# A decoder layer on one core: inputs laid depth-first, the norm applied to the products, and the large projections by Strassen's seven products

## The chip, the cores and the metric

The kernel runs on one core of a Trainium2 chip. The metric is the device time of one execution in microseconds (us), lower is better. The core has five engines that work side by side and wait for each other by semaphores: PE multiplies matrices and writes to PSUM banks of 128 x 512 fp32, DVE and ACT are the vector and the scalar engine, POOL is GpSimd, and SP here does nothing but issue DMAs. Each engine works off its own list of instructions in order.

## The reference

One layer of a decoder, in fp32, with 1024 rows of x and a width of 2048:

```python
h = rmsnorm(x, norm_mix)
(sb_q, sb_k, sb_v, sb_g, gla_q, gla_k, gla_v, gla_r, gla_g, sgu_u, sgu_v, sgu_g) = split(h @ w_in)
o_sb  = stick_breaking_attention(sb_q, sb_k, sb_v)          # 8 heads of 128, strictly causal
o_gla = gla_chunked(gla_q, gla_k, gla_v, log_alpha(gla_r))  # 4 heads
o_sgu = chunked_sgu(gelu(sgu_u), gelu(sgu_v))               # 4 groups of 128
mix = rmsnorm per head of concat(o_sb, o_gla, o_sgu)
x = x + (mix * silu(concat(sb_g, gla_g, sgu_g))) @ w_out
x = x + memory_cross_attention(rmsnorm(x, norm_xattn), rmsnorm(mem, norm_mem))
return rmsnorm(x, final_norm)
```

`w_in` is 2048 x 7184 and `w_out` 2048 x 2048; the memory has 256 rows. In the attention each score row becomes log-probabilities through a running sum from the right end (`suffix`), which is masked so that a row sees only earlier columns.

## The kernel before, in words

**Two parts for each operand.** Every large fp32 operand is split into a float32r tile and the remainder (`split_to`, L142: an ACT cast, L143, then a DVE subtraction, L144). A product of two such pairs is three matmuls (`mm3`, L184). Weights come in pieces of 128 x 512 (256 KB) through `raw_weights` L150 (3 buffers `wraw`) and `weights` L159 (3 buffers `whl` for the two parts). The order of PE's list is written by hand: `weave` (L224) lays the groups of a projection (one weight piece, and the matmuls that use it) in a row and puts each small task before the step that its due time names.

**Stages.** (1) Rows of x arrive, are normed on DVE (L348), and are turned by PE (`flip`, L179) into `hT`, 16 slices of 128 along the depth by two halves of 512 rows, as two parts; meanwhile the first columns of v are computed. (2) `natural` / `row_block` (L269, L242) compute the rest of v, the GLA values and gate and the three SGU inputs, with one k-slice of a 512-column weight at a time into 8 banks; results go to DRAM scratch. (3) Keys and values of the memory. (4) `column_block` (L195) computes transposed products for 128 columns: four groups, each of one weight piece and 24 matmuls. Through it run the gates, GLA's q and k (beside them the SGU tasks, then the GLA tasks from L576 on, whose seven levels per pair of heads are DVE work in `gla_decay`, `gla_factors`, `gla_level`), then q and k of each attention head, always one head ahead of the tasks of `attend` (L831). (5) The output projection goes in four chunks of 512 columns (`mixed` L956 makes the operand from the heads' results and gates, `evac_chunk` L973 adds x). (6) The second norm, the cross-attention and the last norm.

**The attention tasks.** `scores` (L847): three matmuls for a tile of z, then ACT abs, exp and ln (L858 to L860), DVE (L861), for the tile on the diagonal a DVE multiplication by a triangle of ones (L863), the running sum on DVE (L865), a copy of its end on POOL (L869), a DVE subtraction (L871), ACT exp (L872), and a POOL `affine_select` on the diagonal tile (L844). `turn` (L877) transposes the probabilities, `values` (L891) multiplies by v, which POOL's own DMA queue brings (L838), `square` and `close` (L899, L909) norm the head.

**POOL** has little in its list besides: one product of gate and mixer in SGU (L543), GLA (L749) and `mixed` (L970).

```python
def zero_later(dsl):
    pool.affine_select(out=dsl, in_=dsl, pattern=[[-1, P]], compare_op=ALU.is_gt, fill=0.0,
                       base=0, channel_multiplier=1)
...
act.activation(tw, tw, AF.Ln, bias=1.0)
dve.scalar_tensor_tensor(out=tw, in0=z, scalar=0.0, in1=tw, op0=ALU.max, op1=ALU.add)
if diag:
    dve.tensor_tensor(out=t[:, width - P:width], in0=t[:, width - P:width], in1=consts["before"], op=ALU.mult)
```

Of the kernel before, what the change touches and what calls it, by code (L numbers as in the profile page):

```python
# [34 lines left out]
def spread(ap, n):  # L35
    """[p, a] -> [p, a, n], each value n times."""
    p, a = ap.shape
    return ap.unsqueeze(2).to_broadcast([p, a, n])
# [3 lines left out]
def trunk(ctx, tc, x, mem, norm_mix, w_in, w_gla_gate_up, b_gla_gate, sgu_norm, w_sgu, b_sgu,  # L42
          out_norm, w_out, norm_xattn, norm_mem, w_xq, w_xkv, w_xo, final_norm, out, dbg=None):
# [3 lines left out]
    x2d, mem2d, out2d = x[0], mem[0], out[0]  # L47
    w_in3 = w_in[0].rearrange("(k p) n -> p k n", p=P)
# [6 lines left out]
    actp = ctx.enter_context(tc.tile_pool(name="actp", bufs=16))  # L55
    wraw = ctx.enter_context(tc.tile_pool(name="wraw", bufs=3))
# [11 lines left out]
    def slot(dt=F32R, name="slot"):  # L68
        return actp.tile([P, 4, 512], dt, tag="act", name=name)

    class Operand:
        """[2048, 1024] with its first axis on partitions, as two tiles that add up to it, by four k and half."""
# [4 lines left out]
        def fill(self, half):  # L77
            for kg in range(4):
                self.t[kg, half] = (slot(), slot())
# [4 lines left out]
        def group(self, kg, s):  # L84
            c = (s % 4) * P
            return tuple(t[:, :, c:c + P] for t in self.t[kg, s // 4])

    def scratch(name, shape):
# [4 lines left out]
    ident = const.tile([P, P], F32, name="ident")  # L93
    make_identity(nc, ident)
    ones_f = const.tile([P, P], F32, name="ones_f")
    dve.memset(ones_f, 1.0)
    ones_r = const.tile([P, P], F32R, name="ones_r")
    dve.tensor_copy(ones_r, ones_f)
    eps_t = const.tile([P, 1], F32, name="eps_t")
    dve.memset(eps_t, EPS)  # L100

    layout = (("out", out_norm[0], 16), ("xat", norm_xattn[0], 16), ("mem", norm_mem[0], 16), ("bg", b_gla_gate[0], 2),
              ("bs", b_sgu[0], 4))
    cols_at, n_cols = {}, 0
    for nm, _, n in layout:
        cols_at[nm] = n_cols
        n_cols += n
    cols = const.tile([P, n_cols], F32, name="cols")

    def load_cols():  # L110
        """Vectors that act per partition, one column for each 128 values."""
        rows = wraw.tile([P, 512], F32, tag="wr", name="rows")
        for nm, src, n in layout:
            c = cols_at[nm]
# [80 lines left out]
    def column_block(acts, w3, c0, evac, halves=(0, 1)):  # L195
# [6 lines left out]
        def step(kg, kk):  # L202
# [10 lines left out]
            if k == KT - 1:  # L213
                for h in halves:
                    evac(h, banks[h])
# [1003 lines left out]
```

## Time and profile before

| what | value |
|---|---|
| three runs | 2186.28, 2185.3, 2181.64 us; median 2185.3 us |
| profiled execution | span 2184.6 us from the first to the last instruction |
| busy share of the span | PE 97%, DVE 47%, ACT 39%, POOL 7% |
| moved by DMA | 231.18 MB, 106 GB/s over the span |

The profile's span is the nearest figure to a run's time; it lies 0.7 us below the median. "Busy" counts an instruction from its start to its end, and matmuls overlap in PE's pipeline, so a busy PE is not always a PE at full pace. A row of groups names line, engine, operation, output and input, shapes and count, then the busy time in us and the mean of one in ns, then idle time ahead of them and what ended it.

### The profile page before, as it was taken

Reading aid. Unit: us, or ns where it says so; the run is one execution under the profiler, and the core shown is the slowest. Engines: PE = TensorE matmul, PEld = TensorE weight load, DVE = VectorE, ACT = ScalarE, POOL = GpSimd, SP = SyncE. Lnnn points to the kernel's source line nnn. Section 1 sums busy time; section 2 is a strip of 40 time slices with the busy share of each in tenths; the row PEclk is TensorE's granted clock in tenths of the full one; section 3 lists DMA queues with packets and bytes.
Section 4 is the critical chain, followed back from the end, with each engine's and each line's share of the span. In section 5 each row is a group of like instructions: output and inputs, shape, how many; then the busy total and the mean of one; then the engine's idle time right before and its main releaser. Section 6 shows DMA issues by size and latency. Waiting matters only on the chain.

```text
span 2184.6 us, 28465 instructions
## 1 busy us (share of the span) xinstructions
PE 2125.8 (97%) x10525; PEld 1767.4 (81%) x10525; DVE 1020.7 (47%) x1984; ACT 860.9 (39%) x1987; POOL 163.5 (7%) x273
## 2 busy tenths in 40 slices
PE   6999999999999999999999999999989999999997
PEld 6998888888887767878888888888877878888885
DVE  6621211111115627375377677776753121377674
ACT  6421111221215424242356565666654121356552
POOL 2110000000000110101111111111012000000001
PEclk9999999999999999999999999999999999999999
DMA  7541321331317621313222222222267231655632
GB/s 215 151 146 49 126 87 49 97 97 49 98 55 219 184 61 44 107 34 92 78 57 55 56 63 56 61 54 56 83 192 231 69 124 49 207 201 154 216 121 92
DMA packets 181847, 231.18 MB, mean 106 GB/s; under 512 B 17270, under 2 KB 106956, under 8 KB 179532
## 3 DMA queue, kind: packets, MB, share of 16 engines
q1 hardware_dynamic: 170572, 214.68, 32.1%
q0 software_dynamic: 11136, 14.69, 2.6%
q8 instruction: 83, 1.36, 0.3%
q14 instruction: 56, 0.46, 0.1%
HBM read 177.93 MB, written 51.38 MB: 105 GB/s over the span
## 4 chain that ended last, share of the span: by engine, by line
PE 44%; DVE 8%; ACT 5%; issue 4%; DMA 2%; POOL 1%; DVEq 0%; SPq 0%; POOLq 0%; ACTq 0%
PE pj L175 31%; PE z L175 6%; PE av L175 4%; PE tr L180 1%; DVE a L865 1%; DVE a L871 1%; PE tr L175 1%; ACT a L872 1%; DMA mraw<-mix 1%; ACT t L859 1%; ACT t L860 1%; DVE t L861 1%; DVE ql L663 1%; ACT t L858 1%; DVE wl L144 1%
## 5 line engine op out<-in xcount | busy, mean ns | idle before, releaser
L144 DVE TENSOR_TENSOR wl<-wr,wh 128x512 fp32r<-128x512 f32 (+1 forms) x392 | 267.6, 683 | 773.8 <-ACT wh L143 767.6
L175 PE MATMUL pj<-slot,wh 128*128 128x512 f32 x2048 | 576.9, 398 | 1.6 <-DVE qT L144 1.6
L143 ACT CAST wh<-wr 128x512 fp32r<-128x512 f32 (+1 forms) x395 | 237.6, 602 | 798.4 <-PE av L175 548.6
L175 PE MATMUL pj<-wh,slot 128*128 128x512 f32 (+1 forms) x1760 | 500.7, 370 | 0.0
L175 PEld LDWEIGHTS pj<-slot,wh 128*128 128x128 f32 x2048 | 369.7, 188 | 72.4 <-issue 2.3
L175 PEld LDWEIGHTS pj<-wh,slot 128*128 128x128 f32 x1760 | 321.5, 190 | 54.8
L175 PE MATMUL pj<-wl,slot 128*128 128x512 f32 (+1 forms) x880 | 328.9, 374 | 1.7 <-DVE wl L144 1.5
L175 PE MATMUL pj<-slot,wl 128*128 128x512 f32 x1024 | 327.9, 391 | 0.0
L175 PEld LDWEIGHTS pj<-slot,wl 128*128 128x128 f32 x1024 | 192.2, 188 | 42.7
L175 PEld LDWEIGHTS pj<-wl,slot 128*128 128x128 f32 x880 | 167.1, 190 | 30.3 <-DVE wl L144 2.3
L175 PE MATMUL z<-wh,slot 128*128 128x512 f32 x576 | 178.6, 390 | 0.7 <-DVE slot L144 0.7
L175 PEld LDWEIGHTS z<-wh,slot 128*128 128x128 f32 x576 | 108.2, 188 | 24.1 <-DVE slot L144 1.9
L175 PE MATMUL z<-wl,slot 128*128 128x512 f32 x288 | 112.5, 391 | 4.4 <-DVE xo L982 2.7
L861 DVE SCALAR_TENSOR_TENSOR t<-z,t 128x384 f32<-128x384 f32 (+2 forms) x96 | 53.4, 556 | 94.3 <-ACT t L860 94.2
L872 ACT ACTIVATE a<-a 128x384 f32<-128x384 f32 (+2 forms) x96 | 50.4, 525 | 114.5 <-DVE a L871 114.4
L175 PE MATMUL pj<-slot,oT 128*128 128x512 f32 x384 | 92.7, 396 | 0.0
L175 PE MATMUL tr<-wh,slot 128*128 128x512 f32 x288 | 88.7, 389 | 0.0
L175 PE MATMUL av<-wh,slot 128*128 128x512 f32 x288 | 88.7, 389 | 0.0
L175 PEld LDWEIGHTS pj<-slot,oT 128*128 128x128 f32 x384 | 71.0, 188 | 15.7
L175 PE MATMUL z<-kT,qT 128*128 128x512 f32 (+3 forms) x288 | 71.1, 355 | 0.0
L175 PEld LDWEIGHTS z<-wl,slot 128*128 128x128 f32 x288 | 54.0, 188 | 17.2 <-DVE xo L982 3.6
L144 DVE TENSOR_TENSOR aTl<-tr,aTh 128x512 fp32r<-128x512 f32 (+2 forms) x112 | 55.2, 493 | 19.3 <-ACT aTh L143 18.2
(252 smaller groups left out, 2684.2 us busy)
## 6 DMA issues: line engine op xcount, KB each, us to landing
wr<-in_w_in_dram SPq DMA_DIRECT2D x216, 256.0 KB, 2.8
wr<-in_w_out_dram SPq DMA_DIRECT2D x88, 256.0 KB, 2.8
xt<-in_x_dram SPq DMA_DIRECT2D x32, 256.0 KB, 4.8
wr<-in_w_xkv_dram SPq DMA_DIRECT2D x32, 256.0 KB, 3.2
v<-v_scr POOLq DMA_DIRECT2D x64, 128.0 KB, 2.8
xr<-in_x_dram SPq DMA_DIRECT2D x32, 256.0 KB, 5.1
x<-xo SPq DMA_DIRECT2D x32, 256.0 KB, 4.4
x2t<-x SPq DMA_DIRECT2D x8, 1024.0 KB, 7.2
```

The costliest lines, as they stand in the source:

```text
L143: act.copy(hi, src)
L144: eng.tensor_tensor(out=lo, in0=src, in1=f32(hi), op=ALU.subtract)
L175: i = pe.matmul(o, l, r, start=start, stop=stop)
L180: i = pe.transpose(o, i_, ident)
L663: dve.tensor_tensor(out=gl["ql"][r_, :, hh, :].rearrange("p c (b i) -> p c b i", i=h), in0=gl["q"][r_, :].rearrange("p (c b i) -> p c b i" ...
L858: act.activation(tw, z, AF.Abs)
L859: act.activation(tw, tw, AF.Exp, scale=-1.0)
L860: act.activation(tw, tw, AF.Ln, bias=1.0)
L861: dve.scalar_tensor_tensor(out=tw, in0=z, scalar=0.0, in1=tw, op0=ALU.max, op1=ALU.add)
L865: dve.tensor_tensor_scan(out=aw[:, ::-1], data0=tw[:, ::-1], data1=tw[:, ::-1], initial=init, op0=ALU.add, op1=ALU.max)
L871: dve.tensor_tensor(out=aw, in0=z, in1=aw, op=ALU.subtract)
L872: act.activation(aw, aw, AF.Exp)
```

## The change

**Layout.** Three inputs are handed over in another layout: x and memory also with the depth first (`xT`, `memT`), and the short vectors as columns. PE no longer turns x, memory or the vectors. The rms factors are computed beside the first products and applied to the results (`r_all` along the columns, `r_row` and `r_mem` per row). Only the gains are applied to x when a slice is loaded.

**Seven products.** Both operands of a projection are cut into quarters: rows of x in two halves, depth in two halves, columns of the weight in two halves. Strassen's scheme computes seven products of sums of quarters instead of eight products of quarters. `products` (new L290) runs one product over 8 k-slices for two blocks of columns. For each k-slice it loads one or two 128 x 512 weight quarters, adds or subtracts them on POOL (L308), splits the sum (L153 ACT, L154 DVE) and multiplies. `x_load` and `x_sum` (L377, L384) make the operand of the other side, one per round. `Block.evac` adds the products to accumulators in SBUF. v, SGU u and v, GLA v and GLA q, k go this way in seven rounds (products 5, 1, 7, 6, 3, 2, 4).

**Pairs.** The q and k of each of the eight heads, and the 16 gates as eight pairs of 128 columns, go through `pair_steps` (L611) in three sweeps over all 16 pairs: products 2 and 4 (kind 24), 3 and 5 (kind 35), 1, 7 and 6 (kind 176). Sums of weights are on POOL: 128 x 256 (L636) in the first two sweeps, 128 x 384 (L640) in the third. Half-done results wait in DRAM (`part_scr`). `finish` (L558) multiplies by the rms factor on POOL (L559), and for gates forms the silu by three ACT passes and a second POOL product (L565). SGU and GLA tasks run beside the first two sweeps, the attention beside the third, the memory projection and the first rounds of the output projection, which has seven rounds of two blocks of columns (products 7, 4, 2, 3, 5, 1, 6) with accumulators that start as x.

**Smaller edits.** The mask of the scores goes from a DVE product to a second `affine_select` on POOL (L1055). `close` multiplies by ones in plain fp32 instead of two float32r parts, and multiplies by the gate on POOL (L1125). The raw weight buffers go from 3 to 8, the big operand slots from 16 to 8.

```diff
-    wraw = ctx.enter_context(tc.tile_pool(name="wraw", bufs=3))
+    wraw = ctx.enter_context(tc.tile_pool(name="wraw", bufs=8))
...
+    def products(units, sums, spread_out):
...
+        def load(j):
+            for i in range(0 if not j else j + 1, min(j + 2, len(units))):
+                fetch(i)
+            bl, i, k = units[j]
+            r, n = raw.pop(j), bl.width
+            if len(r) == 2:
+                pool.tensor_tensor(out=r[0][:, :n], in0=r[0][:, :n], in1=r[1][:, :n], op=plus_minus(OF_W[i][1][2]))
+            tw[j] = tuple(whl.tile([P, 512], F32R, tag=f"w{x_}", name=f"w{x_}") for x_ in "hl")
+            split_to(tw[j][0][:, :n], tw[j][1][:, :n], r[0][:, :n])
...
+    def x_sum(i, r, pool_, first=False):
...
+            if first and (i, sh, kh) in SQUARED:
+                sq = ev1.tile([P, 512], F32, tag="sq", name="sq")
+                act.activation(sq, t, AF.Square)
+                pool.tensor_tensor(out=squares[:, sh], in0=squares[:, sh], in1=sq, op=ALU.add)
+        if i in (6, 7):
+            pool.tensor_tensor(out=ps[0], in0=ps[0], in1=ps[1], op=ALU.subtract)
+        if i in (1, 2, 5):
+            act.activation(ps[0], ps[0], AF.Copy, scale=g[0])
+            dve.scalar_tensor_tensor(out=ps[1], in0=ps[1], scalar=g[1], in1=ps[0], op0=ALU.mult, op1=ALU.add)
+            split_to(hi, lo, ps[1])
+        else:
+            split_gain(hi, lo, ps[0], g[0])
...
+    PHASES = (5, 1, 7, 6, 3, 2, 4)
...
+    def finish(t, dst, half, silu):
+        pool.tensor_tensor(out=t, in0=t, in1=r_all[:, half * 512:half * 512 + 512], op=ALU.mult)
+        if silu:
+            e = ev_tile()
+            act.activation(e, t, AF.Exp, scale=-1.0)
+            act.activation(e, e, AF.Ln, bias=1.0)
+            act.activation(e, e, AF.Exp, scale=-1.0)
+            pool.tensor_tensor(out=t, in0=t, in1=e, op=ALU.mult)
+        sp.dma_start(dst[:, half * 512:half * 512 + 512], t)
...
+    def evac_176(n, b, st):
+        _, to, silu = PAIRS[n]
+        m1 = ev_tile()
+        act.copy(m1, b[1])
+        for q, i in enumerate((7, 6)):
+            dve.tensor_tensor(out=st[q], in0=b[i], in1=st[q], op=ALU.add)
+        for q in range(2):
+            pool.tensor_tensor(out=st[q], in0=st[q], in1=m1, op=ALU.add)
+            finish(st[q], to[q], q, silu)
...
+            if nk == 2:
+                pool.tensor_tensor(out=t[:, :256], in0=t[:, :256], in1=t[:, 256:], op=ALU.subtract)
+            else:
+                r = t
+                t = ev.tile([P, 3 * P], F32, tag="ts", name="ts", bufs=2)
+                pool.tensor_tensor(out=t, in0=r[:, :3 * P], in1=r[:, P:], op=ALU.add)
+            tw[j] = tuple(whl.tile([P, 512], F32R, tag=f"w{x_}", name=f"w{x_}") for x_ in "hl")
+            split_to(tw[j][0][:, :width], tw[j][1][:, :width], t[:, :width])
...
             if diag:
-                dve.tensor_tensor(out=t[:, width - P:width], in0=t[:, width - P:width], in1=consts["before"], op=ALU.mult)
+                zero_later(t[:, width - P:width])
...
-            for i in range(2):
-                mm(st, ones_r, t[:, i, :], i == 0, i == 1)
+            mm(st, ones_f, sq, True, True)
...
+            pool.tensor_tensor(out=sq, in0=sq, in1=gt, op=ALU.mult)
...
-        natural(mT, w_out3, n * 512, 512, evac_chunk(n), order=order)
+    PHASES_O = (7, 4, 2, 3, 5, 1, 6)
```

POOL's list before, in the attention stage: loads of v (L838), the select on the probabilities (L844) and the copy of a running sum's end (L869) are all there is.

```order
L838 DMA v<-v_scr_92 128x256
L844 AFFINE_SELECT a<-a 128x128 x4
L869 COPY carry<-a 128x1
L838 DMA v<-v_scr_93 128x256
L838 DMA v<-v_scr_94 128x256
```

POOL's list now, in the attention stage, at the end of a pair of gates (`ts` is a sum of weights on its way to PE, `ev` results on their way to DRAM, `sq` a head's normed output, `gt` its gate, `t` and `a` the scores' tiles):

```order
L640 TENSOR_TENSOR ts<-wr 128x384
L604 TENSOR_TENSOR ev<-ev 128x512
L559 TENSOR_TENSOR ev<-ev,r_all 128x512
L604 TENSOR_TENSOR ev<-ev 128x512
L559 TENSOR_TENSOR ev<-ev,r_all 128x512
L640 TENSOR_TENSOR ts<-wr 128x384
L565 TENSOR_TENSOR ev<-ev 128x512 x2
L1047 DMA v<-v_scr_90 128x256
L1055 AFFINE_SELECT t<-t 128x128
L640 TENSOR_TENSOR ts<-wr 128x384
```

The weight sums now stand in one list with the results' products, with two selects for each diagonal tile instead of one, and with the loads of v; the sum for the next weight piece stands behind whatever is ahead of it there.

PE's list before, beside an attention head's values (`pj<-slot` are the projection's matmuls, `av` the values', `tr` the transposes of the probabilities, `z` the scores):

```order
L175 MATMUL pj<-slot,wl 128x512 x2
L175 MATMUL av<-aTl,v 128x256
L175 MATMUL av<-aTh,v 128x256 x2
L175 MATMUL av<-aTl,v 128x128
L175 MATMUL av<-aTh,v 128x128 x2
L175 MATMUL pj<-slot,wh 128x512 x4
```

PE's list now, at such a place:

```order
L185 MATMUL pj<-wh,slot 128x512 x2
L185 MATMUL av<-aTl,v 128x256
L185 MATMUL av<-aTh,v 128x256 x2
L185 MATMUL av<-aTl,v 128x128
L185 MATMUL av<-aTh,v 128x128 x2
L185 MATMUL z<-kT,qT 128x512 x3
L185 MATMUL pj<-wl,slot 128x512
```

The attention's own matmuls are the same; a weight piece now feeds 9 matmuls (three products of one k-slice) where it fed 24.

982 lines of the change are left out of this document (566 added, 416 removed).

## The prediction

> **What bounds the kernel now.** I read the page first, then the clock, then the busy time by stage, then the chain of waits in a stage that looks full, then single stretches of DVE and POOL. The page:
>
> ```profile
> span 2184.6 us, 28465 instructions
> PE 2125.8 (97%) x10525; PEld 1767.4 (81%) x10525; DVE 1020.7 (47%) x1984; ACT 860.9 (39%) x1987; POOL 163.5 (7%) x273
> GB/s 215 151 146 49 126 87 49 97 97 49 98 55 219 184 61 44 107 34 92 78 57 55 56 63 56 61 54 56 83 192 231 69 124 49 207 201 154 216 121 92
> core 0: 2184.6 us, clock 0.996
> ```
>
> The busy time by stage (after the engines: granted clock, DMA share, GB/s):
>
> ```profile
> core 0: us, PE busy (x) PEld busy (x) DVE busy (x) ACT busy (x) POOL busy (x), PEclk, DMA share, GB/s
> 0.00:50.00 50.00, 33.69 (x238) 31.73 (x239) 31.65 (x68) 32.30 (x88) 13.17 (x17) 0.97 0.72 218
> 50.00:100.00 50.00, 48.86 (x408) 47.72 (x409) 34.14 (x83) 25.30 (x74) 6.51 (x10) 1.00 0.54 160
> 100.00:700.00 600.00, 598.71 (x2758) 496.57 (x2757) 111.14 (x185) 127.42 (x226) 7.23 (x12) 1.00 0.32 96
> 775.00:1045.00 270.00, 262.12 (x1314) 210.73 (x1313) 149.29 (x237) 87.75 (x177) 28.91 (x41) 1.00 0.23 66
> 1045.00:1550.00 505.00, 501.67 (x2584) 419.63 (x2583) 340.42 (x653) 296.49 (x660) 61.12 (x155) 1.00 0.23 60
> 1550.00:1665.00 115.00, 107.15 (x492) 86.13 (x491) 63.84 (x106) 62.18 (x121) 22.38 (x21) 0.99 0.56 178
> 2170.00:2185.00 15.00, 0.57 (x3) 0.13 (x1) 4.56 (x9) 1.85 (x5) 1.69 (x1) 0.66 0.18 70
> ...
> 105.00:125.00 20.00, 20.00 (x169) 19.94 (x168) 8.30 (x20) 6.61 (x18) 3.67 (x6) 1.00 0.57 167
> ```
>
> PE is the bound in every stage; DVE reaches two thirds only in the first 100 us and in the attention (340 of 505), and POOL does nothing worth naming: 61 of 505 us there. The kernel has no waits left that could pay for a rewrite; a gain can only come from fewer matmuls. What one costs is seen where PE's chain is unbroken:
>
> ```profile
> 1859.09 54.40 PE pj L175 x240
> ```
>
> That is 54.40 / 240 = 0.227 us for 512 columns; the stretch from 105 us, all of 256 columns, gives 20 / 169 = 0.118, say 0.12.
>
> **What PE loses.** Counted in the two orders, 512-column float32r matmuls fall from 7696 to 6880, 256-column ones from 1456 to 1296, transposes from 732 to 572; 32 256-column matmuls in plain fp32 come on top (the heads' norms). Per transpose and per fp32 matmul:
>
> ```profile
> L180 PE MATMUL tr<-ident,a 128*128 128x128 f32 x288 | 44.5, 273 | 0.0
> L175 PE MATMUL z<-v,kdn 128*128 128x256 f32 x28 | 8.4, 380 | 0.0
> ```
>
> The transposes' busy share is 44.5 / 288 = 0.155 us each, an upper bound since their ends overlap; 128 columns at the pace of 0.227 for 512 would be 0.057, a lower one, and I take 0.1. So: 816 x 0.227 = 185, 160 x 0.12 = 19, 160 x 0.1 = 16, less 32 x 0.38 = 12 and about 3 of small ones: **-205 us**. Strassen saves an eighth of the large projections; that is all of it.
>
> Waits of replaced stages go too. In the first 100 us PE handles 646 matmuls, mostly of 256 columns, where the full rate of 169 in 20 us would need 76; after about 10 us of start it had 90, so 14 were lost. GLA's stretch leaves 270 - 262 = 8, the start of the output projection 115 - 107 = 8. Together **-30**, and 2184.6 - 205 - 30 = 1950 would be the span if every new instruction hid.
>
> **What the others gain.** POOL goes from some 150 us of work to some 950, SP from 865 DMAs to 2315, moved bytes by two. POOL's part matters because it does not run beside DVE freely. DVE and POOL around 720 us, then around 1641 us:
>
> ```profile
> 719.84 0.74 DVE L524 SCALAR_TENSOR_TENSOR sv<-sv,rs_r,gn 128x512 f32<-128x512 f32 x1
> 720.50 1.77 DVE L144 TENSOR_TENSOR wl<-wr,wh 128x512 fp32r<-128x512 f32 x1
> ...
> 720.06 1.66 POOL L543 TENSOR_TENSOR y<-y,sg 128x512 f32<-128x512 f32 x1 [570.56 <-ACT wh L143]
> ```
>
> ```profile
> 1640.57 0.69 DVE L144 TENSOR_TENSOR slot<-mraw,slot 128x512 fp32r<-128x512 f32 x1 [2.83 <-ACT slot L143]
> 1641.62 1.38 DVE L144 TENSOR_TENSOR wl<-wr,wh 128x512 fp32r<-128x512 f32 x1 [0.35 <-ACT wh L143]
> ...
> 1641.15 1.29 POOL L970 TENSOR_TENSOR mraw<-mraw,graw 128x512 f32<-128x512 f32 x1 [1.26 <-ACT graw L969]
> ```
>
> The split that takes 0.69 alone takes 1.77 beside a POOL product, and ends 0.55 after it: the two exclude each other, they do not slow each other. Likewise the POOL product that meets a DVE instruction takes 1.66, not 1.29. So in each stage POOL's tensor instructions and DVE's with two inputs in SBUF form one queue, and where that queue is longer than PE's work, it is the bound. Its prices:
>
> ```profile
> L749 POOL TENSOR_TENSOR og<-og,gg 128x256 f32<-128x256 f32 x16 | 13.4, 841 | 102.8 <-ACT v L748 102.8
> L844 POOL TENSOR_SCALAR_AFFINE_SELECT a<-a 128x128 f32<-128x128 f32 x64 | 19.3, 301 | 193.2 <-ACT a L872 184.1 <-PE pj L175 9.0
> L869 POOL COPY carry<-a 128x1 f32<-128x1 f32 x32 | 9.6, 301 | 139.4 <-DVE a L865 139.4
> L144 DVE TENSOR_TENSOR wl<-wr,wh 128x512 fp32r<-128x512 f32 x360 | 254.1, 706 | 746.4 <-ACT wh L143 740.2 <-DMA xr<-in_x_dram 4.8 <-PE tr L180 0.6
> L144 DVE TENSOR_TENSOR wl<-wr,wh 128x256 fp32r<-128x256 f32 x32 | 13.6, 424 | 27.4 <-ACT wh L143 27.4
> L871 DVE TENSOR_TENSOR a<-z,a 128x384 f32<-128x384 f32 x16 | 8.8, 552 | 2.3 <-POOL carry L869 2.3
> L865 DVE TENSOR_TENSOR_SCAN a<-t,carry 128x512 f32<-128x512 f32 x32 | 41.0, 1281 | 0.6
> L865 DVE TENSOR_TENSOR_SCAN a<-t 128x384 f32<-128x384 f32 x16 | 15.3, 957 | 1.0
> ```
>
> *Seven rounds of w_in.* A round is 240 x 0.227 + 96 x 0.12 = 66 us of PE. The third has 16 weight sums of 512 (1.29) and 16 of 256 (0.84), 8 differences of x and 8 sums of squares on POOL, 55 in all, and 32 splits and 8 of x on DVE, 24: 79, or 12 too long. The first, with 24 sums of squares, is 72. The others lie under 66. **+18** (0 to 40).
>
> *Pairs 24 and 35, with SGU and GLA.* A level of GLA takes PE 1.5 units of 12 matmuls, 18 x 0.227 = 4.1, and 16 small ones of its own, 846.68 - 844.90 = 1.8 by the first two rows here. DVE needs the others:
>
> ```profile
> 844.90 2.02 PE L175 MATMUL z<-ql,d 128*128 128x128 f32 x16
> 846.68 1.18 PE L175 MATMUL pj<-slot,wh 128*128 128x512 f32 x4
> ...
> L653 DVE TENSOR_TENSOR d<-bc 128x1024 f32<-128x1024 f32 x14 | 16.8, 1220 | 0.2
> L663 DVE TENSOR_TENSOR ql<-q,d 64x512 f32<-64x512 f32 x28 | 22.8, 816 | 0.2
> L666 DVE TENSOR_TENSOR d<-d,k 128x1024 f32<-128x1024 f32 x14 | 17.1, 1222 | 7.9 <-ACT k L626 7.8
> L677 DVE COPY_PREDICATED attn<-masks,z 128x512 f32<-128x512 uint8 x28 | 24.4, 901 | 9.1 <-PE z L175 9.1
> ```
>
> that is 1.22 + 1.63 + 1.22 + 1.80 = 5.9, and 1.5 splits (a piece now feeds 12 matmuls, before 24) and evacuations 1.3, 7.2; of POOL's 2.4 about half falls on it: 8.4, so 2.5 x 14 levels = 35. The same reckoning for before (a level is 2.75 steps of 6 matmuls and 1.8, 5.5 us; DVE 5.9 and 0.5) gives 12, where its stretch shows the 8 already taken off. SGU's eight rows may lose one POOL product each, 8 x 1.3 = 10. **+45** (10 to 70).
>
> *Pairs 176, with the attention.* PE has 1248 matmuls of 512 columns (283), 267 of 256 (32) and 35 us of smaller ones: 350. POOL has 128 sums of 384 columns at 1.0 (three quarters of 1.29), 94 wide products at 1.29, 18 of 256 at 0.84, 82 selects at 0.30 and 21 copies: 295. DVE has 127 splits of 384 at 0.55, 28 of 512 at 0.71, 40 of 256 at 0.45 (108) and 61 scans, 60 by the rows above. Whether a scan is excluded too, no row of before shows, since none meets a POOL product. With scans the queue is 463, **+113**; without, 403, +53. I take the first: a scan reads two SBUF inputs as the split does, the nearest row. [...] The mask that leaves DVE (64 x 0.29) only moves within this queue.
>
> *Memory and output rounds.* Queue 86 against PE 62 in the first, 301 against 341 in the second; if the second's slack takes up none of it 24, if all 0: **+12**. A round loads up to 48 pieces of 256 KB in 49 us, 257 GB/s. Accumulating costs DVE one PSUM read per product, not excluded, and lies under 341. The cross-attention stays.
>
> Sum: 1950 + 18 + 45 + 113 + 12 = 2138; the time is the span, which lay 0.7 below the median of the runs. **Forecast 2138**, and from the bounds of its terms 2090 to 2180.
>
> **Rivals.**
>
> *POOL's list runs in order (slower).* The pair's end puts four products, and for gates two more that wait for three ACT passes, between two weight sums; each select waits for a score's ACT and DVE chain. The queue is then never full. With three split buffers PE has two units, about 5 us, of cover; it decides from the point where a stall of POOL's list exceeds that. Per pair the queue alone is 463 / 16 = 29; with a stall of one ACT chain I get 30 for heads, 35 for gates, 8 x 65 = 520 in place of 463, +57, and in the first two sweeps a further 20 at the gates. **2215** (2190 to 2260). For it: 950 us on POOL and the order shown above. Against: due times spread the selects, and a list that is late finds its waits already over. PE's gaps would show at each pair's end. [...] The trace of before shows a lowered clock only at the ends, 0.97 and 0.66.
>
> *PE stays the bound.* The exclusion hides in buffers, scans run free: 1950 + 18 + some 20 to 30 of GLA: **1995** (1965 to 2040). For it: PE's chain is unbroken through 600 us at a DVE of 111. Against: the new queue exceeds PE by arithmetic in one stage even without scans.
>
> *Supply.* Stores and loads share SP's list, where one issue takes 0.38 us in the row here, 2315 of them 880, and fetches stand behind results.
>
> ```profile
> 785.30 0.38 SPq L156 DMA_DIRECT2D wr<-in_w_in_dram  x1
> ```
>
> In the stages' table the first 50 us moved 218 GB/s at a share of 0.72, so full is about 300; 33 MB, counted in the order around the memory stage, need 110 us where PE has 88, +22 over my forecast, and every round may lose a few us more: **2170** (2150 to 2200), and about no change at its end.
>
> **How the numbers follow.** The forecast gets 0.43: its mechanism is in the rows and only the scans are inferred. POOL's order 0.31, PE bound 0.19, supply 0.07. Range 2015 to 2240: it leaves out half of the third case and a fifth of the first rival with what lies beyond both, about 2 in 10. The forecast's own range is 2090 to 2180. A measurement of this kernel can tell about 0.2%, some 4.4 us, from no change. Faster: 0.42 + 0.19 + 0.02 = 0.63. Same: 0.04. Slower: 0.33.
>
> **What would show it.** Right: PE busy near 1900 in sum, gaps grouped in the third sweep, with PE's waits there ending on the weights' splits (DVE) or on the sums (POOL L640), DVE scans and splits longer than 0.55 and 1.28 beside POOL, pairs 28 to 30 us apart. POOL's order: POOL idle at the pairs' ends, waiting for ACT, and pairs 35 apart at gates. PE bound: PE waits under 30 us in the third sweep. Supply: waits that end on the weights' DMA and a DMA share near 1. Wrong: a scan of 1.28 us untouched beside a POOL product, or a clock below 0.99 in the middle.

## The result, and the profile after

The changed kernel takes 2464.1 us in the median of four runs (2462.1 to 2469.8), against 2185.5 for the kernel before: a ratio of 1.128, 95% interval 1.127 to 1.130. It is slower by 279 us; the forecast was 2138, the range ended at 2240.

The page of the changed kernel and its clock:

```profile
span 2460.9 us, 31565 instructions
PE 2082.2 (85%) x9472; PEld 1672.4 (68%) x9472; DVE 1528.6 (62%) x2429; ACT 1128.6 (46%) x2487; POOL 1071.4 (44%) x1057
PEclk9999999998999989998899898988988999989999
DMA  6656657568653554777455555657864586665532
core 0: 2460.9 us, clock 0.934
```

No engine is full. The stages, cut where the seven rounds of w_in end, then the first two sweeps of pairs, the third sweep with the attention, memory and output rounds, and the cross-attention:

```profile
core 0: us, PE busy (x) PEld busy (x) DVE busy (x) ACT busy (x) POOL busy (x), PEclk, DMA share, GB/s
0.00:588.00 588.00, 510.72 (x2410) 410.91 (x2411) 320.72 (x453) 235.44 (x448) 243.32 (x215) 0.97 0.65 199
588.00:1118.00 530.00, 460.58 (x2075) 369.74 (x2074) 353.25 (x553) 235.51 (x520) 238.90 (x229) 0.94 0.62 184
1118.00:1640.00 522.00, 414.66 (x1830) 331.29 (x1831) 335.10 (x497) 275.85 (x607) 348.28 (x383) 0.89 0.57 154
1640.00:2215.00 575.00, 470.39 (x2037) 373.38 (x2036) 361.26 (x581) 262.10 (x587) 230.15 (x224) 0.92 0.67 212
2215.00:2461.00 246.00, 225.87 (x1127) 187.12 (x1125) 158.30 (x347) 119.71 (x327) 10.78 (x8) 0.98 0.43 148
```

Since a busy PE here is not PE at full pace (in an unbroken row of before a matmul of 512 columns is busy for 0.39 us and the next starts after 0.227), I divide PE's time by the starts of its matmuls. Up to the full-speed pace of its shape (0.227 us for 512 columns, from 240 in 54.40 us of before, and 0.119 for 256, from 169 in 20 us) the time from one start to the next is work. What is over counts as lost to the slow clock where the granted clock was 0.5, up to as much again as the work (matmuls of 512 columns start 0.427 us apart there, in the median of 360 in the trace of after), and as waiting otherwise. The split between work and waiting shifts by some 35 us with the pace that is taken for the 128-column matmuls, in both columns of the table alike.

| from the first matmul to the last, us | before | after |
|---|---|---|
| work | 2034 | 1826 |
| waiting | 124 | 502 |
| lost to the half clock | 3 | 110 |
| sum | 2161 | 2438 |

So the matmuls were saved, 208 us against the 205 of the forecast, and 485 us of waits and of slow clock took their place. The 9472 matmuls stand in the same order in nearly all the experiments (e7 and e19 leave out those of the attention, e14 and e17 move some within it), so the stages can be cut at the same matmul in every trace. Stage times in us, from the first matmul:

| run | time | rounds of w_in | pairs 24 | pairs 35 | pairs 176 | memory | output rounds | last |
|---|---|---|---|---|---|---|---|---|
| PE's work in it | | 472 | 195 | 196 | 341 | 61 | 345 | 216 |
| after | 2464 | 577 | 262 | 268 | 522 | 100 | 475 | 234 |
| e1 | 2475 | 573 | 265 | 271 | 528 | 104 | 477 | 232 |
| e2 | 2350 | 527 | 260 | 257 | 500 | 97 | 446 | 234 |
| e3 | 2458 | 581 | 264 | 269 | 521 | 101 | 467 | 233 |
| e4 | 2414 | 579 | 263 | 253 | 489 | 100 | 472 | 235 |
| e5 | 2349 | 535 | 252 | 252 | 495 | 100 | 458 | 233 |
| e6 | 2301 | 523 | 257 | 246 | 462 | 94 | 451 | 234 |
| e7 | 2295 | 578 | 264 | 269 | 443 | 89 | 394 | 234 |
| e8 | 2388 | 519 | 263 | 268 | 524 | 103 | 454 | 233 |
| e9 | 2466 | 578 | 263 | 269 | 521 | 103 | 478 | 233 |
| e10 | 2487 | 579 | 262 | 268 | 529 | 116 | 475 | 233 |
| e11 | 2291 | 521 | 254 | 246 | 461 | 98 | 452 | 234 |
| e13 | 2487 | 583 | 265 | 272 | 527 | 100 | 484 | 233 |
| e14 | 2468 | 585 | 265 | 270 | 527 | 96 | 480 | 234 |
| e15 | 2333 | 511 | 260 | 257 | 506 | 98 | 443 | 233 |
| e16 | 2484 | 577 | 268 | 273 | 531 | 101 | 481 | 231 |
| e17 | 2271 | 521 | 258 | 244 | 440 | 95 | 453 | 233 |
| e18 | 2153 | 491 | 242 | 235 | 446 | 102 | 380 | 231 |
| e19 | 2274 | 581 | 262 | 267 | 414 | 94 | 398 | 232 |

Where the weights make PE wait is plain within the rounds of w_in. The first row below lies in a round whose product has two weight quarters to be summed, the second in the round of product 2, whose weight is a single quarter:

```profile
370.00:440.00 70.00, 62.92 (x304) 50.91 (x303) 42.48 (x68) 25.29 (x48) 24.53 (x24) 0.95 0.74 227
440.00:510.00 70.00, 70.00 (x355) 58.59 (x354) 36.26 (x63) 34.13 (x67) 4.02 (x3) 1.00 0.58 178
```

With 4 us of POOL instead of 25 and fewer loads PE is busy without a break. In the third sweep PE mostly waits for something else: for the attention's split probabilities (`aTl`) and the heads' norm (`sq`), and only then for weights (`wh`, `wl`):

```profile
PE av L185 <- DVE aTl L154: 43.4, 14, 7.6
PE av L185 <- ACT sq L1122: 23.6, 7, 7.0
PE pj L185 <- ACT wh L153: 19.9, 8, 4.8
PE av L185 <- DVE oc L1114: 9.6, 5, 2.5
PE pj L185 <- DVE wl L154: 3.4, 6, 0.8
```

(waited for: us in total, times, longest).

### The profile page after: what moved, and what is told of

Read it like the earlier page. It is cut to its first block, busy times and chain, and to the rows that moved or that the text cites. A ratio compares the mean times of both kernels' runs of the same rounds, so it can differ in the third digit from the quotient of the medians.

```text
span 2460.9 us, 31565 instructions
## 1 busy us (share of the span) xinstructions
PE 2082.2 (85%) x9472; PEld 1672.4 (68%) x9472; DVE 1528.6 (62%) x2429; ACT 1128.6 (46%) x2487; POOL 1071.4 (44%) x1057
## 4 chain that ended last, share of the span: by engine, by line
PE 31%; DMA 22%; DVE 14%; POOL 13%; ACT 8%; issue 7%; SPq 4%; POOLq 0%; DVEq 0%; ACTq 0%
PE pj L185 21%; DMA wr<-in_w_in_dram 9%; PE z L185 5%; DVE wl L154 3%; POOL wr L308 3%; DMA wr<-mx 3%; DMA wr<-in_w_out_dram 3%; SPq L626 2%; PE av L185 2%; POOL ev L559 2%; DVE a L1076 2%; POOL wr L1194 1%; ACT wh L153 1%; DMA xs<-in_xT_dram 1%; PE tr L185 1%
## 5 line engine op out<-in xcount | busy, mean ns | idle before, releaser
L185 PE MATMUL pj<-slot,wh 128*128 128x512 f32 x2000 | 673.4, 419 | 36.8 <-ACT wh L153 33.4
L154 DVE TENSOR_TENSOR wl<-wr,wh 128x512 fp32r<-128x512 f32 (+1 forms) x528 | 411.3, 785 | 329.1 <-ACT wh L153 306.2
L308 POOL TENSOR_TENSOR wr<-wr 128x512 f32<-128x512 f32 (+1 forms) x240 | 289.0, 1207 | 464.0 <-DMA wr<-in_w_in_dram 190.7
L153 ACT CAST wh<-wr 128x512 fp32r<-128x512 f32 (+1 forms) x528 | 298.0, 571 | 388.9 <-PE pj L185 180.4
L185 PE MATMUL pj<-slot,wl 128*128 128x512 f32 x1000 | 412.3, 412 | 9.3 <-DVE wl L154 8.9
L636 POOL TENSOR_TENSOR wr<-wr 128x256 f32<-128x256 f32 x128 | 123.4, 970 | 183.6 <-DMA wr<-in_w_in_dram 132.9
L640 POOL TENSOR_TENSOR ts<-wr 128x384 f32<-128x384 f32 x128 | 147.9, 1158 | 70.6 <-DVE wl L154 37.4
L153 ACT CAST slot<-wr 128x512 fp32r<-128x512 f32 x92 | 57.0, 620 | 167.4 <-POOL wr L1194 122.7
L154 DVE TENSOR_TENSOR slot<-wr,slot 128x512 fp32r<-128x512 f32 x92 | 70.1, 762 | 93.0 <-ACT slot L153 92.5
L154 DVE TENSOR_TENSOR wl<-ts,wh 128x384 fp32r<-128x384 f32 x128 | 93.4, 731 | 50.1 <-ACT wh L153 49.3
L559 POOL TENSOR_TENSOR ev<-ev,r_all 128x512 f32<-128x512 f32 x64 | 94.8, 1481 | 40.4 <-DVE ev L579 34.5
L185 PE MATMUL z<-wh,slot 128*128 128x512 f32 x352 | 112.3, 401 | 0.0
```

The lines of the kernel that those rows point to most:

```text
L153: act.copy(hi, src)
L154: eng.tensor_tensor(out=lo, in0=src, in1=f32(hi), op=ALU.subtract)
L185: i = pe.matmul(o, l, r, start=start, stop=stop)
L308: pool.tensor_tensor(out=r[0][:, :n], in0=r[0][:, :n], in1=r[1][:, :n], op=plus_minus(OF_W[i][1][2]))
L559: pool.tensor_tensor(out=t, in0=t, in1=r_all[:, half * 512:half * 512 + 512], op=ALU.mult)
L636: pool.tensor_tensor(out=t[:, :256], in0=t[:, :256], in1=t[:, 256:], op=ALU.subtract)
```

## The experiments

Theory L is the forecast's, read from a split that took 1.77 us beside a POOL product and 0.69 alone: POOL's instructions that read SBUF and DVE's with two inputs there exclude each other, and this common queue is the bound. Its rivals here: the buffers and loads of the weights (R, D, B) and the cover that split weights give PE (C), the order of POOL's list (Q), SP's list (S), POOL's own occupation (O), the whole path of the weights (W), and the attention's chain (V). "Slower" and "faster" below are against the changed kernel's 2464 us.

**e1: second quarters in buffers of their own.** The reason was this stretch of the chain of waits in a two-quarter round of the changed kernel: sum, load, sum, load, one after the other, 3.10 us for a unit of 256 columns, for which PE needs 12 x 0.12 = 1.44.

```profile
240.51 0.75 POOL wr L308
241.26 0.02 issue
241.28 2.17 DMA wr<-in_w_in_dram
243.45 0.02 issue
243.48 0.04 POOLq L308
243.52 0.09 issue
243.61 0.75 POOL wr L308
```

```diff
-    wraw = ctx.enter_context(tc.tile_pool(name="wraw", bufs=8))
+    wraw = ctx.enter_context(tc.tile_pool(name="wraw", bufs=5))
+    wsec = ctx.enter_context(tc.tile_pool(name="wsec", bufs=3))
...
-                t = raw512()
+                t = second512() if raw[j] else raw512()
```

> The second weight quarter of each sum (and the second piece of each output operand) gets buffers of its own: 5 raw buffers and 3 for second pieces in place of 8 for both, so the second piece's buffer is used again after three sums and not, as in 42 of 312 cases, after one. Theory R (the loads of second quarters go to the one buffer that the sum just before has let go, so load, sum, load, sum run one after the other): the two-quarter rounds of w_in fall from about 85 to about 70 us and the output rounds as much, 2464 goes to 2300 to 2365. Theory L (POOL and DVE exclude each other and that queue is the bound): nothing changes in the queue, 2450 to 2475. Theory Q (POOL's list runs in order and stalls behind results and selects): 2450 to 2475.

Measured: 2474.7, rounds 573. Theory R falls: buffers of their own for the second quarters do not shorten the rounds, so I read the ping-pong as what a starved path looks like. The edit also leaves 5 buffers and not 8 for all first pieces, which costs something by itself (e13).

**e2: weight sums on DVE.** In L308, shown here, and likewise in L636 and L640:

```diff
-                pool.tensor_tensor(out=r[0][:, :n], in0=r[0][:, :n], in1=r[1][:, :n], op=plus_minus(OF_W[i][1][2]))
+                dve.tensor_tensor(out=r[0][:, :n], in0=r[0][:, :n], in1=r[1][:, :n], op=plus_minus(OF_W[i][1][2]))
```

> The 288 sums of weight quarters (512, 256 and 384 columns) are done by DVE and not by POOL. Theory L: the queue gets shorter, since DVE needs 0.69 where POOL needs 1.29: 58 us in the third sweep, 20 in the seven rounds, 20 to 40 in the output rounds, 2464 goes to 2340 to 2390. Theory R: a load still waits for the sum before it, only 0.3 to 0.6 us sooner for each unit: 2410 to 2450. Theory Q: the sums in the third sweep leave the list in which they stand behind results, 2464 goes to 2390 to 2420, all of it in the third sweep.

Measured: 2350.5, 114 faster, as theory L said in sum, but at other places: 50 in the rounds (20 expected), 22 in the third sweep (58 expected).

**e3: the mask back on DVE.** `zero_later(t[...])` becomes the product with a triangle again.

> The mask of the scores goes back to a DVE product with a triangle of ones. Theory Q: a select no longer holds up POOL's list behind a score's ACT chain, and the score no longer waits behind POOL's sums: 30 to 60 us less in the third sweep and the stages behind it, 2400 to 2435. Theory L: the mask only moves within the queue, 0.30 for 0.29: 2455 to 2470. Theory R: unchanged, 2455 to 2470.

Measured: 2458.0, 6 faster, the third sweep 521 for 522. The mask costs nothing that can be told.

**e4: results on DVE.** The four `pool.tensor_tensor` of `finish`, `evac_35` and `evac_176` become DVE's.

> The products and sums of finished results (with the rms factor, with the silu, with the shared product) are done by DVE and not by POOL. Theory L: about 150 of them at 0.69 and not 1.29, 90 us of queue, 56 of these in the third sweep: 2464 goes to 2390 to 2420. Theory Q: the bursts at the ends of pairs leave POOL's list, 2380 to 2410, and in the third sweep PE's waits for the attention fall by half. Theory R: no change in the rounds, up to 20 in the sweeps: 2440 to 2465.

Measured: 2413.5, 51 faster: 33 in the third sweep, 15 in the second. The time lies in theory L's range and just above theory Q's, but the third sweep gained 33 where L had 56, and PE's waits for the attention's values there (those over 0.3 us) fell from 72 to 56 us and not by half, as Q had it. Neither theory is borne out in full.

**e5: writes in place of sums.** This takes the exclusion apart from the time that POOL spends, here in L308:

```diff
-                pool.tensor_tensor(out=r[0][:, :n], in0=r[0][:, :n], in1=r[1][:, :n], op=plus_minus(OF_W[i][1][2]))
+                pool.memset(r[1][:, :n], 0.0)
+                pool.memset(r[0][:, :n], 0.0)
+                pool.memset(r[0][:, :n // 4], 0.0)
```

> The sums of weight quarters are left out; in their place POOL only writes zeros, about as long (1.2, 0.75 and 0.95 us by the rows of memsets before), after the same loads. What reads nothing should not exclude DVE. Theory L (the exclusion of reading POOL and DVE instructions): DVE's splits fall back to 0.70, and most of what moving the sums to DVE gained is gained here, 2464 goes to 2340 to 2400. Theory O (POOL's own occupation and the length of the chain load, sum, cast, subtraction): 2440 to 2470.

Measured: 2349.2, 115 faster, the same as with the sums on DVE. The groups of the changed kernel, with sums (behind the shapes: busy us, mean ns of one):

```profile
L154 DVE TENSOR_TENSOR wl<-wr,wh 128x512 fp32r<-128x512 f32 x416 | 353.6, 855 | 232.7 <-ACT wh L153 210.3 <-issue 4.6 <-POOL ts L640 4.3
L1076 DVE TENSOR_TENSOR_SCAN a<-t 128x512 f32<-128x512 f32 x16 | 26.8, 1673 | 10.9 <-POOL t L1055 10.9
```

and of e5, where POOL writes:

```profile
L154 DVE TENSOR_TENSOR wl<-wr,wh 128x512 fp32r<-128x512 f32 x416 | 303.0, 733 | 240.4 <-ACT wh L153 215.5 <-POOL wr L643 4.3 <-POOL wr L638 3.9
L1080 DVE TENSOR_TENSOR_SCAN a<-t 128x512 f32<-128x512 f32 x16 | 21.8, 1359 | 9.2 <-POOL t L1059 9.2
L638 POOL MEMSET wr<- 128x512 f32 x128 | 67.2, 525 | 191.5 <-DMA wr<-in_w_in_dram 154.2 <-ACT ev L578 14.7 <-DVE y L783 9.7
L643 POOL MEMSET wr<- 128x512 f32 x128 | 67.1, 526 | 47.7 <-DMA wr<-in_w_in_dram 44.7 <-issue 2.9
```

The splits fall from 855 to 733 ns, the scans from 1673 to 1359. POOL is busy for 965 us against 1071; part of the difference is time in which the sums had been blocked (in the changed kernel one of 384 columns takes 1.00 us where no DVE instruction runs beside it, and 1.16 in the mean), part is that the writes are somewhat shorter (0.53 and 0.42 us in place of that sum). So the exclusion is real and worth up to 115 us. But it was not the bound of the third sweep: with 128 sums out of its queue the sweep still takes 495.

**e6: sums and results on DVE**, e2 and e4 together.

> Weight sums and results' products both on DVE. Theory L: the two gains of 114 and 50 us add, since POOL then excludes almost nothing: 2285 to 2320. Theory O: POOL is nearly empty and its list no longer orders anything, but DVE's list takes its place, at 1.6 ms of work: 2320 to 2370. In both it stays slower than before.

Measured: 2300.8: the gains add (114 + 51 = 165, measured 163), at DVE 73% busy and POOL 14%. Still 5% slower than before.

**e7: no attention.** `attend` only copies gates.

> The attention is left out (scores, running sums, transposes, products with v, the heads' norm); each head's gate is copied to where its result would go. PE loses about 160 us of work. Theory L: the third sweep still has a queue of 128 + 121 + 95 = about 350 us, so it takes 340 to 370 in place of 522. Theory Q (PE's list waits for the attention's chain through ACT, DVE and POOL, and the weights suffer little): it takes 270 to 310, near PE's 265. In the seven rounds nothing changes.

Measured: 2294.7; the third sweep takes 443, with PE's work there down to 261. Neither theory expected that much. The waits of 300 us of it, engine by engine, and POOL at the end of a pair:

```profile
PE pj L185 <- ACT wh L153: 62.7, 26, 8.1
```

```profile
ACT wh L153 <- POOL ts L640: 172.4, 78, 8.3
```

```profile
POOL ts L640 <- DMA wr<-in_w_in_dram: 62.7, 45, 3.5
POOL ev L604 <- DVE ev L602: 34.0, 9, 5.6
```

```profile
SPq L566 <- POOL ev L565: 37.3, 10, 7.3
SPq L566 <- POOL ev L559: 28.4, 10, 5.1
```

```profile
1315.31 1.26 POOL L604 TENSOR_TENSOR ev<-ev 128x512 f32<-128x512 f32 x1 [3.26 <-DVE ev L602]
1316.53 0.99 POOL L640 TENSOR_TENSOR ts<-wr 128x384 f32<-128x384 f32 x1
1317.48 1.27 POOL L559 TENSOR_TENSOR ev<-ev,r_all 128x512 f32<-128x512 f32 x1
```

POOL stands 3.26 us in a result's sum that needs the pair's last matmul, with the next weight sum behind it: the first rival's mechanism, seen. e10 and e19 price it. A second mechanism is in the same rows: POOL's weight sums wait longer for their loads (62.7 us) than POOL does for results (34.0), and SP, which issues these loads, stands for 66 us at the stores of results (L566) until POOL's products are done, with loads behind them in its list. No run takes this order of SP's list apart.

**e8: half the weight loads.** `OF_W[i][:1]` is loaded, and added to itself.

> In the rounds of w_in and w_out the second weight quarter is not loaded; the sum adds the first to itself, on POOL as before. Theory D (loads: volume, the order of SP's list, the buffers): the two-quarter rounds of w_in fall from about 85 to about 70 us, the output rounds too, 2464 goes to 2300 to 2360. Theory L and theory O: the sums are still there, 2430 to 2465.

Measured: 2387.9, 76 faster: 58 in the rounds of w_in, 21 in the output rounds, nothing elsewhere. Loads are a cause of their own there; e8 also lets the ring of raw buffers reach twice as far ahead, which e13 looks at.

**e9: half the issues in the third sweep.**

```diff
-             176: (((1, 1), (7, 0), (6, 2)), ((1, 0), (1, 1), (0, 0), (0, 1)), 1, evac_176, 1)}
+             176: (((1, 1), (7, 2), (6, 0)), (1, 0), 1, evac_176, 1)}
...
+            if nk == 1:
+                for q, ch in enumerate(quarters_):
+                    c = PAIRS[n][0][ch]
+                    sp.dma_start(r3[:, q::2], w_in3[:, u::8, c:c + P])
+                return
```

> In the third sweep the four 64 KB loads of a weight piece become two of 128 KB with the same bytes (both halves of the depth in one), so SP issues about 256 DMAs fewer there. Without the attention SP had needed 6.25 us for 12 such loads, 2.1 for each unit of 2.04 us of PE. Theory S (SP's list is the bound of the third sweep): 522 us there go to 450 to 490. Theory Q (POOL's list runs in order, and results at the ends of pairs hold up the weight sums) and theory L (exclusion): 515 to 525.

Measured: 2465.5, the sweep 521. The number of SP's issues is not what the sweep waits for. PE's waits for the cast weights (`wh`) there fall from 19.9 to 8.6 us all the same, and the sweep is no shorter: beside the attention these weights came sooner for nothing.

**e10: results later in POOL's list.**

```diff
+        def rest(q):
+            tc.keep_in_program_order(pool.tensor_tensor(out=st[q], in0=st[q], in1=m1, op=ALU.add))
+            finish(st[q], to[q], q, silu)
...
+            if 1 < n < 15:
+                late.append([2 + 2 * q, lambda q=q: rest(q)])
```

> In the third sweep the sums and products of a finished pair's results are placed in POOL's list behind the weight sums of the next pair's first units, one half two units later and one four, for pairs 2 to 14; the work is the same. Theory Q: about 3 us for each of 13 pairs, 522 goes to 475 to 495. Theories L and S: 515 to 525.

Measured: 2487.0, 23 slower: the sweep 529, 7 longer, and the memory stage behind it 116, 16 longer. With the attention beside it the order of results and weight sums gains nothing.

**e11: e6 and e9 together.**

> Weight sums and results on DVE (2301 us) and the loads of the third sweep halved in number. With POOL out of the way, theory S says that SP's list now ends last: the third sweep goes from 462 to 400 to 430, in all 2240 to 2270. If DVE's chains or the attention's order in PE's list end last, 2290 to 2305. In both it stays slower than before.

Measured: 2291.5 after 2300.8, the sweep 461 for 462: theory S, as a matter of the number of issues, falls again.

**e13: six raw buffers.**

> 6 raw weight buffers in place of 8, nothing else. Theory B (the loads of the two-quarter rounds cannot run far enough ahead; the gain of the halved loads was that of a ring twice as deep): the seven rounds and the output rounds get 20 to 60 us longer each, 2500 to 2560. If the buffers are not what holds the loads up: 2455 to 2480.

Measured: 2487.3, 23 slower, spread over the stages (6 in the rounds, 9 in the output rounds). The depth of the ring matters a little. Two buffers fewer cost the rounds 6 us, which speaks against the depth as the source of e8's 58; a deeper ring was not tried.

**e14: values later.** `LAG_V` from 2 to 4.

> The attention's products with v come four steps after their transposes in PE's list and not two; nothing else is moved. Theory V (in the third sweep PE's list calls for the values before ACT, DVE and POOL have made them, 72 of 120 us of long waits there): these waits fall to 20 to 40 us, the sweep from 522 to 460 to 490, in all 2400 to 2435. If the chain as a whole is too slow for its rate and not late by a fixed time, the waits move to the next place (the norm, the scores, the transposes) and the time stays 2450 to 2475.

Measured: 2467.7. The waits of values fall from 72 us (those over 0.3 us, by the matmul that comes late) to 28, and come back as 23 at the transposes, 22 at the norm and 16 at the scores: the chain is too slow for its rate and not late by a fixed time.

**e15: half the loads and sums on DVE.**

> No second weight quarter in the rounds (the first is added to itself) and all weight sums on DVE. Halved loads alone took 58 us from the seven rounds, sums on DVE 50. Theory W (the rounds wait for weights alone, whose path is load, sum, cast, subtraction): both together bring the rounds from 577 to 480 to 500, within 5% of PE's 472, and the clock stays up. If something else holds the rounds: above 510. In all 2290 to 2330.

Measured: 2332.8; the rounds 511, which by the expectation (480 to 500, or above 510 if something else holds them) means that the weights are not all of it. There are 37 us of waits and 3 of half clock left above PE's 472; e18 shows how much of that the rest of the path still holds (491). Of the two savings of 58 and 50 only 66 remain together: each relieves the same path.

**e16: four split buffers, six raw.**

> 4 buffers for finished weight parts and 6 raw ones, where it was 3 and 8 (the same memory). Theory C (PE's cover is short: a stall of the weight path reaches PE after two units): one unit more of cover takes 20 to 50 us from the rounds and sweeps, 2410 to 2445, though six raw buffers alone had cost 23. If the path is too slow on average and not by bursts: 2475 to 2495.

Measured: 2484.2, as with six raw buffers alone (2487). More cover in front of PE gains nothing that can be told; the path is too slow on average.

**e17: e11 and e14 together.**

> Weight sums and results on DVE, half the issues in the third sweep, and the values four steps after their transposes. If the late values are a cause of their own, 20 to 40 us come off 2291: 2250 to 2270; if DVE's list is now what they wait for, 2280 to 2300. Slower than before in both.

Measured: 2270.7, 21 faster than e11, all of it in the third sweep (440 for 461). What the later values could not give by themselves in e14 they give here, with sums and results off POOL's list. This is the fastest version that computes everything; it is still 3.9% slower than the kernel before (ratio 1.039, 1.037 to 1.040).

**e18: no weight path.**

```diff
-            tw[j] = tuple(whl.tile([P, 512], F32R, tag=f"w{x_}", name=f"w{x_}") for x_ in "hl")
-            split_to(tw[j][0][:, :n], tw[j][1][:, :n], r[0][:, :n])
+            tw[j] = zero, zero
```

> The weights of the rounds and of the pairs are not loaded, summed or split; PE multiplies by one constant tile of zeros, in the same order. All else stays (x, attention, SGU, GLA, results, memory; 6 raw buffers). Theory W (the path of the weights is what the new kernel waits for): the seven rounds fall to 475 to 500, the third sweep to 380 to 430, the output rounds to 360 to 400, and the time to 2000 to 2090, below before: the matmuls saved show. If the attention's chain by itself holds up PE's list, the third sweep stays above 450.

Measured: 2152.5, ratio to before 0.986 (0.982 to 0.990). The stages of e18, and PE's longest waits in its third sweep:

```profile
0.00:503.00 503.00, 482.49 (x2408) 401.88 (x2409) 164.98 (x232) 133.09 (x227) 63.87 (x55) 0.99 0.25 83
503.00:979.00 476.00, 442.27 (x2074) 358.67 (x2073) 241.04 (x426) 165.71 (x396) 119.64 (x104) 0.98 0.43 138
979.00:1425.00 446.00, 388.28 (x1833) 316.90 (x1832) 232.03 (x367) 215.46 (x475) 186.24 (x251) 0.94 0.32 100
1425.00:1907.00 482.00, 438.58 (x2033) 356.39 (x2032) 271.94 (x470) 203.75 (x476) 113.21 (x144) 0.98 0.47 147
```

```profile
PE av L187 <- DVE aTl L156: 39.1, 15, 6.1
PE av L187 <- ACT sq L1107: 7.4, 7, 2.9
PE z L187 <- ACT qT L1020: 5.8, 1, 5.8
```

The path of the weights, with all that its loads cost the DMA engines and SP's list, is worth 312 us: 86 in the rounds, 54 in the first two sweeps, 76 in the third, 95 in the output rounds. Without any of it the third sweep still takes 446, and the longest waits there end on the attention's own steps. And it gives back only 33 us against the kernel before: of the 208 us of matmuls saved, 175 are still spent elsewhere.

**e19: no attention, results later.**

> Without the attention as in e7, and with the finished results behind the next pair's weight sums in POOL's list as in e10. Theory Q, now where nothing else can hide it (in e7 POOL waited 3.4 us at the ends of pairs in a result's sum while the next weight sum stood behind it): the third sweep falls from 443 to 340 to 380, in all 2190 to 2235. If that order is not what the weights wait for: 430 to 445, 2285 to 2300.

Measured: 2273.7, 21 faster than e7, the sweep 414 for 443. Moving the results costs nothing and gains 28 us there, about 2 for each pair, where the attention does not hide it. Most of the weights' waits remain: POOL's weight sums still wait 104 us of the 414 for their loads (100 of 443 in e7).

## Why the prediction was wrong

The step that failed is the one under "What the others gain": *where that queue is longer than PE's work, it is the bound*, and else PE is. It takes each stage as limited by one full list. No such list was full. By its own numbers the third sweep's queue is 463 us of a measured 522, 89%, and yet taking 128 sums out of it (e5) brought 27. What the runs showed in its place are chains of hops between lists that are each partly empty: the path of the weights, worth 312 us (e18), and beside it the SGU, GLA and attention chains.

The terms below compare the time of a stage with PE's work in it, as the forecast's terms did. Its base of 1950 still held some 95 us of the waits of before, so the excesses measured here, 612 us in all with the cross-attention, are to be set against its 188 and these 95. The 30 us that it took off for old waits cannot be told apart in them.

**PE's saving: right.** -208 measured for -205.

**The exclusion: right, scans included.** A scan of 512 columns in the changed kernel beside a weight sum, DVE first, then POOL; it takes 2.01 us, where the rows before had 1.28, and ends 1.07 us after the sum, so all but about 0.2 us of its work came behind it:

```profile
1253.44 2.01 DVE L1076 TENSOR_TENSOR_SCAN a<-t,carry 128x512 f32<-128x512 f32 x1
```

```profile
1252.97 1.41 POOL L640 TENSOR_TENSOR ts<-wr 128x384 f32<-128x384 f32 x1
```

What adds to a product in PSUM was not held up, as the forecast had it: of the 16 such sums of L592 in the changed kernel 13 ran beside a product or sum of POOL's for 0.6 us or more and took 0.68 to 0.69 us; the two with none beside them took 0.67 and 0.68.

The price of all exclusion by weight sums is at most 115 us (e5), about what the forecast charged to the third sweep alone; but only 27 of it lie there, and 42 lie in the rounds, where the forecast had 18.

**The rounds, +18: 105 measured** (577 for 472). The weights' path is 86 of it (e18). What it consists of overlaps: loads 58 (e8), sums off POOL 50 (e2) or replaced by writes 42 (e5), loads and sums together 66 (e15). The path has four hops, load, sum, cast, subtraction, on four in-order lists, and each of three edits to a hop (e2, e5, e8) shortened the rounds though DVE, ACT and POOL were each busy for 55% of them or less; the forecast priced one hop, and only where its queue exceeded PE.

**The first two sweeps, +45: 139 measured** (530 for 391). e18 splits it: 54 from the weights, and 85 that stay without them, where the forecast had 45 for SGU and GLA. That these two chains hold all of the 85 is argued and not shown: no run leaves them out.

**The third sweep, +113: 181 measured** (522 for 341), 39 of it the half clock. Two paths cross the same lists, and each alone takes as long: 443 without the attention, 446 without the weights. The right term is not one queue but two chains: the attention's alone misses PE's time by about 100 us, the weights' alone by about 180, and they share ACT, DVE and POOL. Why each needs so long by itself stays open. For the attention, e14 only moved its waits, and in e17 later values took 21 us off a sweep of 461. For the weights, e19 settles 28 us, and the order of SP's list is not tested.

**Memory and output rounds, +12: 170 measured** (575 for 405). Summed queues were the wrong measure here too; 95 of it are the weights' path in the output rounds (e18), 21 of these the loads (e8).

**The clock: not priced** in the sum, 110 us. The clock fell to 0.89 in the third sweep, and a clock below 0.99 in the middle was one of the forecast's own signs of being wrong. Each of the first four stages lost some (granted clock 0.97, 0.94, 0.89 and 0.92 in the stages' table): in the changed kernel some 2.1 us of idle PE within a window of 3.41 us were enough to halve the clock of the next (last section). A small misreading beside it: the trace of before has a lowered clock not only at its ends, since the row from 1550 us shows 0.99.

**The rivals.** The first, POOL's order, was nearest in sign and time (2215), and its mechanism is in the trace, but where a run tested it it was worth 28 us without the attention (e19) and nothing beside it (e10), so its nearness is luck in part. PE as the bound was wrong: even without weights the kernel takes 2153. Supply was right as a cause (76 us in e8) but put in the wrong place: its 22 us were around the memory stage, and e8 gained in the rounds and the output rounds.

So the 208 us saved on PE were outspent: 175 by what stays without the weights' path (e18), and 312 by that path itself. Each piece of weights now feeds 9 or 12 matmuls where it fed 24, and most are loaded as two or four quarters, summed, and then split as before.

## What to carry to other kernels

When a change buys matmuls with work on other engines, price the whole path of one unit (load, sum, cast, subtraction) against PE's time for that unit, and leave slack in every list; a stage can be far from PE's time with every other engine under 70% (here the third sweep, 522 us for 341 of PE's work, with POOL busy for 67%, DVE for 64% and ACT for 53%). Before trusting such a change, run it once with the path left out (e18): here that came out 1.4% faster than before, as a bound for what a better path could bring with the rest as it is. A wait of PE can cost more than its length: here 110 us of slow clock came with 502 us of waits.

## What the runs showed of the hardware

In the changed kernel's trace the granted clock changes only on a fixed grid of 3.41 us (each of the 720 windows cut on it shows 1.00 or 0.50), and what it becomes follows how long PE was idle in the window before. Some of the changed kernel's windows, cut on that grid (PE busy comes first; the third number from the end is the clock of the window):

```profile
267.65:271.06 3.41, 1.66 (x6) 0.98 (x6) 2.89 (x4) 2.14 (x4) 1.84 (x2) 1.00 0.79 240
271.06:274.47 3.41, 3.06 (x13) 2.29 (x14) 1.58 (x3) 1.24 (x2) 3.28 (x3) 1.00 0.78 241
284.71:288.13 3.42, 3.42 (x16) 2.61 (x14) 0.00 (x0) 0.04 (x1) 1.85 (x2) 1.00 0.83 229
288.13:291.54 3.41, 1.41 (x7) 1.05 (x7) 1.35 (x2) 1.19 (x2) 1.65 (x2) 1.00 0.84 260
291.54:294.96 3.42, 3.16 (x8) 1.96 (x6) 0.87 (x1) 1.23 (x2) 1.21 (x2) 0.50 0.85 276
294.96:298.37 3.41, 1.79 (x8) 1.48 (x9) 3.41 (x4) 1.23 (x2) 2.20 (x2) 1.00 0.70 195
```

1.66 us of busy PE in the first window kept the clock; 1.41 in the fourth halved it for the next. From the first matmul to the last some 620 windows of this trace are at full clock, and 63 of them were followed by a half one. By the pace of the matmuls these 63 had PE idle for 2.0 us or more, and no other window was idle for more than 2.14. Out of a half window the way back takes more: with a matmul there counted at twice its full-speed time (0.427 us measured for 512 columns, against 0.227), the 63 that were followed by full clock had PE idle for 0.83 us at most, the 29 that were not for 0.83 or more. Both limits come to about the same work, an estimate of 1.3 us at full pace in a window (3.41 - 2.1, and half of 3.41 - 0.83). In this trace each of the 38 waits of over 3 us cost a slow window, and of the 74 of 0.5 to 1.5 us hardly any did (6). The windows at half clock add up to 325 us, against 19 before.

Two engines' lists that wait for each other do not look busy: in e7 POOL is busy for 59% of the third sweep, DVE for 29%, ACT for 25%, and PE still waits or runs slowly for 181 of 443 us.
